# Moving the RMS scale of a hybrid decoder layer behind its input projection

## The chip, the cores and the metric

The kernel runs on one core of one Trainium2 chip. The metric is the device time of one execution in microseconds (us), the median of several runs. A profiled execution is one run with the hardware profiler on; its span goes from the first to the last instruction.

## The reference, cut to what matters

The input `x` has 2048 tokens of 1024 float32 values. What is computed:

```python
h = rmsnorm(x, norm_pre_g)                     # x * rsqrt(mean(x*x) + eps) * g, per token
z = einsum('bsd,de->bse', h, w_in)             # 1024 -> 4096 columns
q, k, v, g_attn, c_h, c_b, c_c, g_conv = split(z)   # 4 x 768, 4 x 256
q, k = rope(q, pos), rope(k, pos)              # 12 heads of 64
o = 3 dilated windows (128,1) (512,4) (2048,16), mixed by their softmax denominators
attn_out = o * silu(g_attn)
conv_out = c_b * causal_depthwise_conv(c_c * c_h, conv_w) * silu(g_conv)   # width 3
y = einsum('bse,ed->bsd', concat([attn_out, conv_out]), w_out)
out = x + rmsnorm(y, norm_post_g)
```

The RMS factor is one number per token, so it can be applied to `h` before the projection or to each column of `z` after it.

## The kernel before, in words

**Arithmetic.** float32 operands are split into a high part (the float32r cast) and a low part (the rest); a product is three matmuls, high·high, high·low, low·high.

**Tiling.** The tokens are cut into 4 chunks `b` of 512 tokens. The 4096 columns are cut into 8 groups of 512: group 0 and group 7 are convolution groups (c_h, c_c, c_b, gate, 128 columns each), groups 1 to 6 are attention groups (k, q, v, gate of two heads). A unit `n` is one group and one chunk, so there are 32 units, `n = 4 * group + b`: units 0 to 3 and 28 to 31 are convolution units, units 4 to 27 attention units. A unit's projection fills four PSUM tiles `z` (tokens along the free dimension) with 96 matmuls of 512 columns (L816 to L818).

**Start.** `x_chunk(b)` loads four tiles of 128 tokens (L417, 512 KB each), sums their squares on ScalarE (L419), takes the reciprocal root, multiplies the tile by it on VectorE (L428 for chunk 0, L435 for the others), and transposes it on TensorE (L443) into eight tiles; ScalarE writes the high part (L448), VectorE the low part (L450) of `xt`. These are also written to DRAM (L453) and read again for each later group (L459). `weights_in` loads 256 KB of weights (L396, L400) into one of three `raw` tiles and splits them (L403, L404).

**An attention unit.** ScalarE copies k and q out of PSUM (L520); four small transfers each swap the halves of the heads (L523); `rotate` multiplies by the rotary table `cs` (L535, read by L515 into a ring of one buffer) and adds (L539); the results are split (L545, L546 for k; L550, L551 for q). ScalarE copies v out of PSUM (L527), TensorE transposes it (L567). `silu2` takes the gate from PSUM: Tanh on ScalarE (L465), then `(tanh + 1) * z` on VectorE (L466). Scores (L604, L632), maxima and exponentials (L611, L615, L639, L643), transposes of the probabilities (L657), their split (L662, L663), products with v (L676), gathering (L694 to L696), weights over the windows (L742 to L758), and the mixed result `m` (L780 to L783) that goes to DRAM (L784).

**A convolution unit** copies c_h to `hh` (L481) and c_b to `bb` (L490), makes `u = z * hh` (L482), runs the three taps (L492, L494), multiplies by `bb` (L496, GpSimd) and by the gate (L497), and writes the result (L499).

**Output stage.** When all attention results are written, the attention buffers are given up (`open_out`), w_out is loaded (L855) and split (L857, L858), the mixed results are loaded (L867) and split (L868, L869) and projected (L883 to L885). The loads land in 12 tiles: 4 `uu`, 3 `raw` and 5 `ro`.

**Order.** `add(engine, duration, priority, function, reads, writes)` only records an operation. `Plan.schedule` plays all of them through with estimated durations and latencies: an engine that is free takes the ready operation with the smallest priority number whose buffers are free. `URG` marks evictions that go first. Then each engine gets its instructions in the planned order, which is fixed, and all transfers go through the one queue of SP in planned order. A `Ring` gives its buffers in the order in which they were asked for in the code.

## Time and profile before

| what | value |
|---|---|
| time before, median of 3 runs | 1248.66 us (1248.54 to 1251.12) |
| profiled execution, its own time | 1251.67 us |
| span of the profiled execution | 1249.9 us |
| mean granted TensorE clock | 0.992 |
| busy: TensorE, weight loads, VectorE, ScalarE, GpSimd | 1216.9, 1010.9, 826.6, 704.5, 252.5 us |

A busy share is an average over stages. Matmuls are pipelined, so a busy TensorE is not one at its peak; what counts is where its queue waits. Releasers ("<-") are inferred from semaphore events. PE is TensorE, PEld its weight loads, DVE VectorE, ACT ScalarE, POOL GpSimd, SP the engine whose queue issues the transfers (SPq).

### The profile page before, as it was taken

The numbers are of one execution on the slowest core, as the hardware profiler recorded it, in microseconds if no ns is written. First come the engines' busy times: TensorE is split into PE (matmuls) and PEld (weight loads), VectorE is DVE, ScalarE is ACT, GpSimd is POOL, SyncE is SP. The second block draws the span as 40 slices with busy tenths as digits, with TensorE's granted clock in tenths as the row PEclk, the third lists the DMA queues.
The fourth block names the chain that finished last, engine by engine and source line by source line (L and its number), as shares of the span: only waits on it lengthen the run. The fifth ranks groups of instructions, "written<-read, shape, count | busy, mean of one in ns | idle before, by whom it ended". The sixth has DMA issues, their size and how long they took to land.

```text
span 1249.9 us, 20939 instructions
## 1 busy us (share of the span) xinstructions
PE 1216.9 (97%) x6920; PEld 1010.9 (81%) x6920; DVE 826.6 (66%) x2124; ACT 704.5 (56%) x1856; POOL 252.5 (20%) x204
## 2 busy tenths in 40 slices
PE   6999999999999999999999999999999998999997
PEld 5888788888887888888887888888887886788886
DVE  6554367877788777877788677876787535444343
ACT  6533366766776766766766766767665614232121
POOL 0000132322322222322223222312232111000000
PEclk9999899999999999999999999999999999899999
DMA  9847666765777656765777656765778458553331
GB/s 350 326 189 294 227 207 193 248 195 165 240 236 264 222 189 218 241 204 156 239 246 264 214 176 216 262 197 161 233 241 277 131 171 328 186 167 119 101 101 67
DMA packets 137244, 264.39 MB, mean 212 GB/s; under 512 B 31280, under 2 KB 71344, under 8 KB 137136
## 3 DMA queue, kind: packets, MB, share of 16 engines
q1 hardware_dynamic: 137136, 263.07, 63.5%
q8 instruction: 54, 0.88, 0.3%
q14 instruction: 54, 0.44, 0.1%
HBM read 202.51 MB, written 47.91 MB: 200 GB/s over the span
## 4 chain that ended last, share of the span: by engine, by line
PE 83%; DVE 7%; ACT 4%; DMA 2%; issue 2%; SPq 1%; POOL 1%; DVEq 0%; ACTq 0%; POOLq 0%
PE z L816 15%; PE z L818 14%; PE z L817 14%; PE st L676 6%; PE st L657 6%; PE st L884 5%; PE st L885 5%; PE st L883 5%; PE st L604 4%; PE st L632 3%; PE st L443 1%; PE st L816 1%; PE st L818 1%; DVE rp L535 1%; PE st L817 1%
## 5 line engine op out<-in xcount | busy, mean ns | idle before, releaser
L816 PE MATMUL z<-xt,w 128*128 128x512 f32 x960 | 396.7, 413 | 0.0
L818 PE MATMUL z<-xt,w 128*128 128x512 f32 x960 | 376.9, 393 | 0.0
L817 PE MATMUL z<-xt,w 128*128 128x512 f32 x960 | 376.0, 392 | 0.0
L818 PEld LDWEIGHTS z<-xt,w 128*128 128x128 f32 x960 | 180.5, 188 | 41.4
L816 PEld LDWEIGHTS z<-xt,w 128*128 128x128 f32 x960 | 181.1, 189 | 32.2 <-issue 3.0
L817 PEld LDWEIGHTS z<-xt,w 128*128 128x128 f32 x960 | 181.4, 189 | 26.9
L663 DVE TENSOR_TENSOR pt<-st,pt 128x512 fp32r<-128x512 f32 x216 | 142.7, 679 | 57.1 <-ACT pt L662 56.1
L662 ACT CAST pt<-st 128x512 fp32r<-128x512 f32 x216 | 120.2, 579 | 32.4 <-PE st L657 30.3
L676 PEld LDWEIGHTS st<-pt,v 128*128 128x128 f32 x852 | 121.0, 189 | 17.7 <-issue 5.5
L676 PE MATMUL st<-pt,v 128*128 128x256 f32 x852 | 131.7, 285 | 2.4 <-DVE pt L663 2.4
L615 ACT ACTIVATE p<-p,sm 128x128 f32<-128x128 f32 (+3 forms) x192 | 105.7, 553 | 46.4 <-DVE sm L611 46.4
L696 DVE TENSOR_TENSOR uu<-st,uu 64x256 f32<-64x256 f32 x192 | 80.2, 421 | 73.4 <-ACT uu L695 63.8
L657 PE MATMUL st<-cst,p 128*128 128x128 f32 x852 | 122.6, 273 | 0.0
L725 POOL TENSOR_TENSOR uu<-uu 128x512 f32<-128x512 f32 x48 | 67.1, 1398 | 238.3 <-DVE uu L696 238.3
L657 PEld LDWEIGHTS st<-cst,p 128*128 128x128 f32 x852 | 100.5, 140 | 16.7 <-issue 1.5
L643 ACT ACTIVATE p<-p,e 128x256 f32<-128x256 f32 (+1 forms) x192 | 94.8, 497 | 26.3 <-DVE e L639 26.3
L694 ACT COPY uu<-st 64x256 f32<-64x256 f32 x192 | 70.3, 368 | 66.2 <-PE st L676 59.4
L889 ACT ACTIVATE y<-st 128x512 f32<-128x512 f32 x32 | 19.1, 598 | 133.0 <-PE st L885 133.0
L611 DVE CUSTOM_DVE_ANT_0 p<-st,cst 128x128 f32<-128x128 f32 (+3 forms) x192 | 82.1, 486 | 11.1 <-PE st L604 11.0
L639 DVE CUSTOM_DVE_ANT_0 p<-st,cst 128x256 f32<-128x256 f32 (+1 forms) x192 | 66.8, 410 | 21.3 <-PE st L632 21.3
L884 PE MATMUL st<-wo,w 128*128 128x512 f32 x192 | 76.1, 396 | 0.0
L883 PE MATMUL st<-wo,w 128*128 128x512 f32 x192 | 75.8, 395 | 0.0
(135 smaller groups left out, 1763.5 us busy)
## 6 DMA issues: line engine op xcount, KB each, us to landing
xt<-xt SPq DMA_DIRECT2D x256, 512.0 KB, 5.8
raw<-in_w_in SPq DMA_DIRECT2D x64, 256.0 KB, 5.7
cs<-in_rope SPq DMA_DIRECT2D x24, 512.0 KB, 6.4
rp<-rp SPq DMA_DIRECT2D x192, 64.0 KB, 2.0
vd<-v SPq DMA_DIRECT2D x96, 128.0 KB, 4.8
v<-vd SPq DMA_DIRECT2D x24, 512.0 KB, 4.1
ab<-ad SPq DMA_DIRECT2D x48, 256.0 KB, 6.0
mix<-m SPq DMA_DIRECT2D x32, 256.0 KB, 2.2
```

The lines of the kernel that those rows point to most:

```text
L611: add("DVE", dvet(w) + 0.01, pr + URG, lambda h=h, r=r, P4=P4: vec.tensor_tensor_reduce(P4.ap[:, r, 0:w], ps[h].ap[:, (r - r0) * w:(r - r0 ...
L615: add("ACT", actt(w) + 0.19, pr, lambda h=h, r=r, P4=P4: act.activation(P4.ap[:, r, 0:w], P4.ap[:, r, 0:w], AF.Exp, bias=s4(0, h)[:, r:r + ...
L643: add("ACT", actt(256 - lo[g]) + 0.19, pr, lambda h=h, g=g, P1=P1: act.activation(P1.ap[:, g, lo[g]:], P1.ap[:, g, lo[g]:], AF.Exp, bias=E ...
L657: nc.tensor.transpose(ps.ap[:, i * 128:(i + 1) * 128], pp.ap[:, a, c * 128:(c + 1) * 128], ident)
L662: add("ACT", actt(m * 128, True), pr + URG, lambda: act.copy(pt.ap[:, :m, 0, :], p4()), r=[ps], w=[(pt, 0)])
L663: add("DVE", dvet(m * 128), pr + URG, lambda: vec.tensor_tensor(pt.ap[:, :m, 1, :], p4(), f(pt.ap[:, :m, 0, :]), op=ALU.subtract), r=[ps, ...
L676: mm(dst, v, pt.ap[:, i], start=s, stop=e)
L816: mm(z.ap, w.ap[:, 0, js], xt.ap[:, 0], start=kt == 0, stop=False)
L817: mm(z.ap, w.ap[:, 0, js], xt.ap[:, 1], start=False, stop=False)
L818: mm(z.ap, w.ap[:, 1, js], xt.ap[:, 0], start=False, stop=kt == KT - 1)
L883: mm(z.ap, m.ap[:, 0, il], wo[:, 0, dl], start=e == 0, stop=False)
L884: mm(z.ap, m.ap[:, 0, il], wo[:, 1, dl], start=False, stop=False)
```

## The change

The projection takes `x * g` without the RMS factor. Tiles of x are transposed as they land. Chunk 0 is loaded in eight halves of 256 KB, first the columns of the first four transposes, behind the identity and the first weights. The squares are summed later; the factor of 512 tokens is spread over the 128 partitions by four transposes of a broadcast column (`spread`) and stands as a third plane of the table `t`; the rotary planes are multiplied by it. The table of a chunk goes to DRAM (`t_d`, 768 KB) and is read again for every later unit. In the units v, the gate, c_h and c_b are multiplied by the plane on VectorE as they leave PSUM, `u` once more on GpSimd. `silu2` writes the scaled gate, takes Tanh from it into an `rp` tile, and multiplies. The first eight weights land in `raw`, `rp` and `g` tiles. `g` has three tiles instead of two, `m` none: mixed results are written over the gates. The output stage's loads land in `uu`, `raw`, `rp` and `g` (14 tiles) instead of 12. The ring `sm` has three tiles instead of four.

```diff
+    t_d = [dram.tile([128, 3, C], F32, name=f"t{b}") for b in range(NB)]
...
-    g_r = ring(cp, "g", 2, [128, C])
+    g_r = ring(cp, "g", 3, [128, C])
-    m_r = ring(cp, "m", 2, [128, C])
+    raw0_r = Ring(list(raw_r) + list(rp_r) + list(g_r)[:1])
...
-    cs_r = ring(ap_, "cs", 1, [128, 2, C], F32, "STREAM")
+    cs_r = ring(cp, "cs", 1, [128, 3, C], F32, "STREAM")
-    sm_r = ring(ap_, "sm", 4, [128, 64])
+    sm_r = ring(ap_, "sm", 3, [128, 64])
-    junk = cs_r[0].ap.rearrange("p a b -> p (a b)")
+    junk = ab_r[0].ap.rearrange("p a b c -> p (a b c)")
...
-        pr = (4 * grp - 1) * 100 + 50 + 6 * i if grp else -150 + 5 * i
-        raw, w = Tok(raw_r), Tok(wp_r)
+        pr = (4 * grp - 1) * 100 + 50 + 6 * i if grp else -150 + 5 * i if i else -161
+        pc = pr if grp else URG + (-150 + 5 * i if i < 4 else 45.6 + i)
+        raw, w = Tok(raw_r if grp else raw0_r), Tok(wp_r)
-        add("ACT", actt(C), pr, lambda: act.copy(w.ap[:, 0], raw.ap), r=[raw], w=[(w, 0)])
-        add("DVE", dvet(C) + 0.07, pr, lambda: vec.tensor_tensor(w.ap[:, 1], raw.ap, f(w.ap[:, 0]), op=ALU.subtract),
+        add("ACT", actt(C), pc, lambda: act.copy(w.ap[:, 0], raw.ap), r=[raw], w=[(w, 0)])
+        add("DVE", dvet(C) + 0.07, pc, lambda: vec.tensor_tensor(w.ap[:, 1], raw.ap, f(w.ap[:, 0]), op=ALU.subtract),
             r=[raw, (w, 0)], w=[(w, 1)], after=XL[i - 1:i] if grp == 0 and i else ())
...
-    XT, XL = {}, []
     def x_chunk(b):
-        pr = b * 100 - 60 if b else -200
+
         xn = []
-        root = Tok(sm_r) if b else None
+        root, tp, t = Tok(sm_r), Tok(st_r), Tok(cs_r)
+        T[b] = t
         for i in range(4):
-            t = Tok(xs_r)
-            rows = slice(b * C + i, (b + 1) * C, 4)
-            add("DMA", dmat(512), b * 100 - 160 + i, lambda t=t, rows=rows: nc.sync.dma_start(t.ap, x[rows]), w=[t])
-            s, k = (root, i) if b else (Tok(sm_r), 0)
-            add("ACT", actt(D), pr + i, lambda t=t, s=s, k=k: act.activation(junk, t.ap, AF.Square, accum_out=s.ap[:, k:k + 1]),
-                r=[t], w=[(s, k), "junk"])
-            if b == 0:
-                add("ACT", 0.2, pr + i, lambda s=s: act.activation(s.ap[:, 3:4], s.ap[:, 0:1], AF.Sqrt, bias=eps, scale=1.0 / D),
-                    r=["eps", (s, 0)], w=[(s, 3)])
-                add("DVE", 0.07, pr + i, lambda s=s: vec.tensor_scalar(
-                    s.ap[:, 1:2], s.ap[:, 0:1], 1.0 / D, EPS, op0=ALU.mult, op1=ALU.add), r=[(s, 0)], w=[(s, 1)])
-
-                def norm(t=t, s=s):
-                    vec.tensor_scalar(t.ap, t.ap, rsqrt_root(s.ap), None, op0=ALU.mult)
-                add("DVE", 1.5, pr + i, norm, r=[s], w=[t])
-            xn.append(t)
-        if b:
-            after = XL[4:5] if b == 1 else ()
-            add("DVE", 2.6, pr + 4, lambda: rsqrt_mean(root.ap), w=[root], after=after)
-            for i, t in enumerate(xn):
-                add("DVE", 0.75, pr + 4 + i, lambda i=i, t=t: vec.tensor_scalar(
-                    t.ap, t.ap, root.ap[:, 8 + i:9 + i], None, op0=ALU.mult), r=[root], w=[t])
+            xn.append(Tok(xs_r))
+        rows = [slice(b * C + i, (b + 1) * C, 4) for i in range(4)]
+        for h in range(2):
+            for i, z in enumerate(xn):
+                pr = -160 + h * 7 + i if b == 0 else b * 100 - 160 + i
+                if b == 0:
+                    add("DMA", dmat(256), pr, lambda z=z, i=i, h=h: nc.sync.dma_start(
+                        z.ap[:, h * C:(h + 1) * C], x[rows[i], h * C:(h + 1) * C]), w=[(z, h)], land=4.0)
+                elif h == 0:
+                    add("DMA", dmat(512), pr, lambda z=z, i=i: nc.sync.dma_start(z.ap, x[rows[i]]), w=[(z, 0), (z, 1)])
...
             pos = 8 * b + kt - 4
-            p2 = pos // 8 * 100 + 49.5 + pos % 8 if pos >= 0 else -100 + kt
-            xpre = add("PE", 0.44, p2, tr, r=xn + ["cst"], w=[ps, (s, "hold")])
-            x_last.append(xpre)
+            p2 = pos // 8 * 100 + 49.5 + pos % 8 if pos >= 0 else -152 + 5 * kt
+            x_last.append(add("PE", 0.44, p2, tr, r=[(z, kt // 4) for z in xn] + ["cst"], w=[ps, (s, "hold")]))
...
-            add("DMA", dmat(512), p2 + 60, lambda kt=kt, s=s: nc.sync.dma_start(xt_d[b][kt], f(s.ap)), r=[s], w=[("xt", b, kt)])
+            add("DMA", dmat(512), max(p2, -50) + 60, lambda kt=kt, s=s: nc.sync.dma_start(xt_d[b][kt], f(s.ap)), r=[s], w=[("xt", b, kt)])
+        pr = b * 100 - 40
+        for i, z in enumerate(xn):
+            x_last.append(add("ACT", actt(D), pr + i, lambda i=i, z=z: act.activation(junk, z.ap, AF.Square, accum_out=root.ap[:, i:i + 1]),
+                              r=[z], w=[(root, i), "junk"], after=XL[3:4]))
+        pr += 8
+        add("DVE", 2.6, pr, lambda: rsqrt_mean(root.ap), w=[root])
+
+        def spread():
+            for i in range(4):
+                nc.tensor.transpose(tp.ap[:, i * 128:(i + 1) * 128], root.ap[:, 8 + i:9 + i].to_broadcast([128, 128]), ident)
+        add("PE", 0.44, pr, spread, r=[root, "cst"], w=[tp, (t, "hold")])
+        add("ACT", actt(C, True), pr + URG, lambda: act.copy(t.ap[:, 2], tp.ap), r=[tp], w=[(t, 2)])
+        add("DMA", dmat(512), b * 100 - 50, lambda: nc.sync.dma_start(t.ap[:, 0:2], rope[b]), w=[(t, 0)])
+        for i in range(2):
+            add("DVE", dvet(C), pr + 10, lambda i=i: vec.tensor_tensor(t.ap[:, i], t.ap[:, i], t.ap[:, 2], op=ALU.mult), r=[(t, 2)], w=[(t, 0)])
+        add("DMA", dmat(768), pr + 60, lambda: nc.sync.dma_start(t_d[b], t.ap), r=[t], w=[("t", b)])
+
+    T = {}
 
     def x_stream(n, kt):
...
-    def silu2(z, pr):
-
-        g = Tok(g_r)
-        add("ACT", actt(C, True), pr, lambda: act.activation(g.ap, z.ap, AF.Tanh, scale=0.5), r=[z], w=[g])
-        add("DVE", dvet(C) + 0.07, pr, lambda: vec.scalar_tensor_tensor(g.ap, g.ap, 1.0, z.ap, op0=ALU.add, op1=ALU.mult),
-            r=[z], w=[g])
+    def silu2(z, t, pr):
+
+        g, th = Tok(g_r), Tok(rp_r)
+        add("DVE", dvet(C), pr, lambda: vec.tensor_tensor(g.ap, z.ap, t.ap[:, 2], op=ALU.mult), r=[z, t], w=[g])
+        add("ACT", actt(C), pr, lambda: act.activation(th.ap, g.ap, AF.Tanh, scale=0.5), r=[g], w=[th])
+        add("DVE", dvet(C) + 0.07, pr, lambda: vec.scalar_tensor_tensor(g.ap, th.ap, 1.0, g.ap, op0=ALU.add, op1=ALU.mult),
+            r=[th], w=[g])
         return g
+
+    def table(b, prio):
+
+        t = Tok(cs_r)
+        add("DMA", dmat(768), prio, lambda: nc.sync.dma_start(t.ap, t_d[b]), r=[("t", b)], w=[t])
+        return t
...
-        hh, bb, y, m = Tok(rp_r), Tok(rp_r), Tok(rp_r), Tok(m_r)
-        add("ACT", actt(C, True), pe, lambda: act.copy(hh.ap, zs[0].ap), r=[zs[0]], w=[hh])
+        t = table(b, pr - 100) if i else T[b]
+        hh, bb = Tok(rp_r), Tok(rp_r)
+        add("DVE", dvet(C), pe, lambda: vec.tensor_tensor(hh.ap, zs[0].ap, t.ap[:, 2], op=ALU.mult), r=[zs[0], (t, 2)], w=[hh])
         add("DVE", dvet(C), pe, lambda: vec.tensor_tensor(
             u.ap[:, 2:].rearrange("p r i -> p (r i)"), zs[1].ap, hh.ap, op=ALU.mult), r=[zs[1], hh], w=[(u, 1)])
+        add("POOL", poolt(C), pe, lambda: pool.tensor_tensor(
+            u.ap[:, 2:].rearrange("p r i -> p (r i)"), u.ap[:, 2:].rearrange("p r i -> p (r i)"), t.ap[:, 2], op=ALU.mult), r=[t], w=[(u, 1)])
 
...
-        add("ACT", actt(C, True), pe, lambda: act.copy(bb.ap, zs[2].ap), r=[zs[2]], w=[bb])
-        g = silu2(zs[3], pe)
+        add("DVE", dvet(C), pe, lambda: vec.tensor_tensor(bb.ap, zs[2].ap, t.ap[:, 2], op=ALU.mult), r=[zs[2], (t, 2)], w=[bb])
+        g = silu2(zs[3], t, pe)
+        y = Tok(rp_r)
...
-        add("DVE", dvet(C) + 0.07, pr, lambda: vec.scalar_tensor_tensor(m.ap, y.ap, 0.5, g.ap, op0=ALU.mult, op1=ALU.mult),
-            r=[y, g], w=[m])
-        add("DMA", dmat(256), pr, lambda: nc.sync.dma_start(mix_d[6 + i][b], m.ap), r=[m], w=[("mix", 6 + i, b)])
+        add("DVE", dvet(C) + 0.07, pr, lambda: vec.scalar_tensor_tensor(g.ap, y.ap, 0.5, g.ap, op0=ALU.mult, op1=ALU.mult),
+            r=[y], w=[g])
+        add("DMA", dmat(256), pr, lambda: nc.sync.dma_start(mix_d[6 + i][b], g.ap), r=[g], w=[("mix", 6 + i, b)])
...
-        cs = Tok(cs_r)
-        add("DMA", dmat(512), pr - 100, lambda: nc.sync.dma_start(cs.ap, rope[b]), w=[cs], after=x_last)
+        cs = table(b, pr - 100)
...
-        add("ACT", actt(C, True), pe + 2, lambda: act.copy(vz.ap, zs[2].ap), r=[zs[2]], w=[vz])
-        gs = silu2(zs[3], pe + 3)
+        add("DVE", dvet(C), pe + 2, lambda: vec.tensor_tensor(vz.ap, zs[2].ap, cs.ap[:, 2], op=ALU.mult), r=[zs[2], cs], w=[vz])
+        gs = silu2(zs[3], cs, pe + 3)
...
-        add("POOL", poolt(C), pr, lambda: pool.tensor_tensor(m.ap, a4.ap, gs.ap, op=ALU.mult), r=[a4, gs], w=[m])
-        attn_last.append(add("DMA", dmat(256), pr, lambda: nc.sync.dma_start(mix_d[p][b], m.ap), r=[m], w=[("mix", p, b)]))
+        add("POOL", poolt(C), pr, lambda: pool.tensor_tensor(gs.ap, a4.ap, gs.ap, op=ALU.mult), r=[a4], w=[gs])
+        attn_last.append(add("DMA", dmat(256), pr, lambda: nc.sync.dma_start(mix_d[p][b], gs.ap), r=[gs], w=[("mix", p, b)]))
...
-    add("DMA", 0.5, -156.5, lambda: nc.sync.dma_start(ident, consts[:, 0:128]), w=["cst"])
-    add("DMA", 1.2, 0, lambda: nc.sync.dma_start(cst[:, 128:], consts[:, 128:]), w=["masks"])
-    add("DMA", 0.5, -156.4, lambda: nc.sync.dma_start(gp, g_pre), w=["gp"])
+    add("DMA", 0.5, -165, lambda: nc.sync.dma_start(ident, consts[:, 0:128]), w=["cst"])
+    add("DMA", 0.5, -156.5, lambda: nc.sync.dma_start(gp, g_pre), w=["gp"])
+    add("DMA", 1.2, 200, lambda: nc.sync.dma_start(cst[:, 128:], consts[:, 128:]), w=["masks"])
     add("DMA", 0.5, -100, lambda: nc.sync.dma_start(cw, conv_w), w=["cw"])
-    for b in range(NB):
-        x_chunk(b)
     for n in range(8 * NB):
         grp, b = divmod(n, NB)
+        if n < NB:
+            x_chunk(b)
...
-    ro_r = Ring([Slot() for _ in range(5)])
-    or_r = uu_r + raw_r + ro_r
+    or_r = uu_r + raw_r + rp_r + g_r
```

## Rows read from the trace of the kernel before

**Rows 1.** The page, busy time of each engine over the span.
```profile
PE 1216.9 (97%) x6920; PEld 1010.9 (81%) x6920; DVE 826.6 (66%) x2124; ACT 704.5 (56%) x1856; POOL 252.5 (20%) x204
```

**Rows 2.** Busy time by stretch: the stretch in us, its length, busy us of PE, PEld, DVE, ACT and POOL with their instructions, granted clock, DMA share, GB/s.
```profile
125.00:150.00 25.00, 23.12 (x116) 18.85 (x114) 9.41 (x33) 8.46 (x29) 5.08 (x4) 0.86 0.74 257
...
600.00:800.00 200.00, 198.57 (x1240) 166.10 (x1237) 153.62 (x418) 138.91 (x387) 51.82 (x43) 1.00 0.68 219
...
1050.00:1100.00 50.00, 42.74 (x175) 34.14 (x174) 24.08 (x50) 17.97 (x37) 2.81 (x1) 0.90 0.61 215
```

**Rows 3.** Waits of TensorE's matmuls over the whole span: who waited for whom, us in total, times, longest.
```profile
PE st L883 <- ACT mx L868: 4.4, 1, 4.4
PE st L885 <- DVE mx L869: 2.9, 1, 2.9
PE st L604 <- DVE q L551: 2.6, 5, 0.6
PE st L567 <- ACT rp L527: 2.5, 2, 1.9
```

**Rows 4.** The chain of waits in the first 17 us, in order of time: start, us, what.
```profile
0.74 4.07 DMA p<-in_x
4.83 1.16 ACT cs L419 x2
...
11.85 0.77 DVE p L428
...
12.66 3.46 PE st L443 x17
16.12 0.23 PE z L816
```

**Rows 5.** The timeline at the start: start, us, engine, line, operation, tiles, count, idle before and releaser. Two lines of SP's queue and TensorE's first transposes.
```profile
0.74 1.81 SPq L417 DMA_DIRECT2D p<-in_x  x4
2.59 0.66 SPq L791 DMA_DIRECT2D cst<-in_consts  x1
...
8.98 1.04 PE L443 MATMUL st<-cst,p 128*128 128x128 f32 x2 [8.98 <-DMA cst<-in_consts]
```

**Rows 6.** What the transfers moved in the first 20 us, in 40 slices of 0.5 us.
```profile
GB/s 0 0 0 106 49 295 360 410 426 418 434 401 410 442 370 370 379 406 389 390 382 401 393 328 393 385 410 369 418 401 434 391 416 420 428 393 426 434 410 410
```

**Rows 7.** The chain of waits from 0 to 40 us: one group of four transposes of x once the projection runs.
```profile
18.86 0.44 PE st L443 x4
```

**Rows 8.** Single lines over the whole span: engine, operation, count, duration in ns as least/median/most, first and last start, shape.
```profile
L663 DVE TENSOR_TENSOR pt<-st,pt x216: 545/691/694, 152.6 to 999.2; 128x512 fp32r<-128x512 f32 x108
L466 DVE SCALAR_TENSOR_TENSOR g<-g,z x24: 677/687/690, 141.0 to 953.5; 128x512 f32<-128x512 f32 x24
L535 DVE TENSOR_TENSOR rp<-rp,cs x72: 651/691/1802, 131.1 to 940.9; 128x512 f32<-128x512 f32 x72
L539 POOL TENSOR_TENSOR rp<-rp,rp x24: 1288/1542/1782, 137.7 to 942.3; 128x512 f32<-128x512 f32 x24
L527 ACT COPY rp<-z x24: 579/587/590, 139.9 to 952.2; 128x512 f32<-128x512 f32 x24
L419 ACT ACTIVATE cs<-p x12: 1038/1058/1080, 4.8 to 58.6; 128x1024 f32<-128x1024 f32 x12
L419 ACT ACTIVATION_READ_ACCUMULATOR cs<-p x12: 182/186/223, 5.8 to 59.5; 128x1 f32 x12
```

**Rows 9.** The timeline where the scores of the second attention unit of a group of four begin: start, us, engine, line, idle before and releaser.
```profile
597.65 0.59 ACT L527 COPY rp<-z 128x512 f32<-128x512 f32 x1
597.66 1.11 DVE L551 TENSOR_TENSOR q<-rp,q 128x512 fp32r<-128x512 f32 x1 [1.33 <-ACT q L550]
...
598.80 0.69 DVE L466 SCALAR_TENSOR_TENSOR g<-g,z 128x512 f32<-128x512 f32 x1
...
598.83 0.62 PE L604 MATMUL st<-kk,q 64*128 64x256 f32 x6 [0.52 <-DVE q L551]
```

**Rows 10.** The timeline at the end of the first attention unit's projection.
```profile
138.26 0.39 PE L818 MATMUL z<-xt,w 128*128 128x512 f32 x1
...
139.36 0.62 ACT L550 CAST q<-rp 128x512 fp32r<-128x512 f32 x1 [5.58 <-POOL rp L539]
139.89 0.58 ACT L527 COPY rp<-z 128x512 f32<-128x512 f32 x1
...
140.52 0.66 PE L567 MATMUL st<-cst,rp 128*128 128x128 f32 x4 [1.88 <-ACT rp L527]
```

**Rows 11.** The rotary table: the page's row of its transfers (KB each, median us from issue to landing), and SP's queue from one unit's load to the next unit's swaps.
```profile
cs<-in_rope SPq DMA_DIRECT2D x24, 512.0 KB, 6.4
...
595.18 0.38 SPq L515 DMA_DIRECT2D cs<-in_rope  x1
...
615.62 2.45 SPq L523 DMA_DIRECT2D rp<-rp  x4
```

**Rows 12.** The beginning of the output stage: SP's queue, and two lines of ScalarE's timeline.
```profile
1033.13 0.38 SPq L850 DMA_DIRECT2D gpost<-in_g_post  x1
1040.25 0.32 SPq L499 DMA_DIRECT2D mix<-m  x1
1040.62 2.34 SPq L855 DMA_DIRECT2D ro<-in_w_out  x5
...
1055.16 0.59 ACT L481 COPY rp<-z 128x512 f32<-128x512 f32 x1 [3.70 <-PE z L818]
```

More of the change, by code (lines that the diff above doesn't have):

```diff
@@ L315, in hybrid_layer @@
     cw = cp.tile([128, 2, 3], F32, name="cw")
-    eps = cp.tile([128, 1], F32, name="eps")
-    eps2 = cp.tile([128, 1], F32, name="eps2")
+    t_d = [dram.tile([128, 3, C], F32, name=f"t{b}") for b in range(NB)]
     xt_d = [[dram.tile([128, 2, C], F32, name=f"xt{b}_{k}") for k in range(KT)] for b in range(NB)]
@@ L405, in weights_in @@
             r=[raw, (w, 0)], w=[(w, 1)], after=XL[i - 1:i] if grp == 0 and i else ())
-    XT, XL = {}, []
+    XT, XL, x_last = {}, [], []
     def x_chunk(b):
-        pr = b * 100 - 60 if b else -200
         xn = []
-        root = Tok(sm_r) if b else None
+        root, tp, t = Tok(sm_r), Tok(st_r), Tok(cs_r)
+        T[b] = t
         for i in range(4):
-            t = Tok(xs_r)
-            rows = slice(b * C + i, (b + 1) * C, 4)
-            add("DMA", dmat(512), b * 100 - 160 + i, lambda t=t, rows=rows: nc.sync.dma_start(t.ap, x[rows]), w=[t])
-            s, k = (root, i) if b else (Tok(sm_r), 0)
-            add("ACT", actt(D), pr + i, lambda t=t, s=s, k=k: act.activation(junk, t.ap, AF.Square, accum_out=s.ap[:, k:k + 1]),
-                r=[t], w=[(s, k), "junk"])
-            if b == 0:
-                add("ACT", 0.2, pr + i, lambda s=s: act.activation(s.ap[:, 3:4], s.ap[:, 0:1], AF.Sqrt, bias=eps, scale=1.0 / D),
-                    r=["eps", (s, 0)], w=[(s, 3)])
-                add("DVE", 0.07, pr + i, lambda s=s: vec.tensor_scalar(
-                    s.ap[:, 1:2], s.ap[:, 0:1], 1.0 / D, EPS, op0=ALU.mult, op1=ALU.add), r=[(s, 0)], w=[(s, 1)])
-                def norm(t=t, s=s):
-                    vec.tensor_scalar(t.ap, t.ap, rsqrt_root(s.ap), None, op0=ALU.mult)
-                add("DVE", 1.5, pr + i, norm, r=[s], w=[t])
-            xn.append(t)
-        if b:
-            after = XL[4:5] if b == 1 else ()
-            add("DVE", 2.6, pr + 4, lambda: rsqrt_mean(root.ap), w=[root], after=after)
-            for i, t in enumerate(xn):
-                add("DVE", 0.75, pr + 4 + i, lambda i=i, t=t: vec.tensor_scalar(
-                    t.ap, t.ap, root.ap[:, 8 + i:9 + i], None, op0=ALU.mult), r=[root], w=[t])
@@ L452, in x_chunk @@
                 r=[ps, "gp", (s, 0)], w=[(s, 1)]))
-            add("DMA", dmat(512), p2 + 60, lambda kt=kt, s=s: nc.sync.dma_start(xt_d[b][kt], f(s.ap)), r=[s], w=[("xt", b, kt)])
-    x_last = []
+            add("DMA", dmat(512), max(p2, -50) + 60, lambda kt=kt, s=s: nc.sync.dma_start(xt_d[b][kt], f(s.ap)), r=[s], w=[("xt", b, kt)])
[15 more added lines that the diff above has]
+    T = {}
     def x_stream(n, kt):
@@ L777, in weight @@
             return ab.ap[:, i].rearrange("p g (r j) -> p g r j", r=4)
-        a4, a1, m = UU[4][0], UU[1][0], Tok(m_r)
+        a4, a1 = UU[4][0], UU[1][0]
         add("DVE", dvet(C), pr, lambda: vec.tensor_tensor(rows(a4), rows(a4), weight(1), op=ALU.mult), r=[ab], w=[a4])
@@ L837, in open_out @@
         for s, t in zip(xr_r, ring(op_, "xr", 2, [128, D])):
-            s.ap = t.ap
-        for s, t in zip(ro_r, ring(op_, "ro", 5, [128, C])):
             s.ap = t.ap
```

2 lines of the change are left out of this document (removed).

## The prediction

> **What bounds the kernel now.** I read the busy times first, then the busy times by stretch, then TensorE's waits, and last the chain of waits at the places where the waits lie. TensorE is busy for 97% of the span [rows 1], which alone says little, since its matmuls are pipelined; but its waits over the whole span are short and few: the longest are 4.4, 2.9, 2.6 and 2.5 us in total, 12.4 us of 1249.9 [rows 3]. In a stretch of 200 us amid the attention units TensorE shows 198.57 us, VectorE 153.62 (77%) and ScalarE 138.91 (69%) [rows 2]. So TensorE's queue sets the time from its first projection to the end, and three places lie outside that: the head, where the first projection starts only at 16.12 us [rows 4]; the first attention unit, where the granted clock of the stretch falls to 0.86 [rows 2, 10]; and the beginning of the output stage with 7.3 us of waits and a granted clock of 0.90 [rows 2, 3]. An edit pays only if it shortens one of these or takes instructions off TensorE; work on other engines costs nothing until TensorE waits for it.
>
> **The head: the largest term.** Before, the chain is: x lands at 4.81 us; squares, root and product of one tile after another; the last product at 11.85; then the transposes from 12.66, 17 in 3.46 us, and the projection at 16.12 [rows 4]. The change takes squares, root and products out of it. What is left is the landing of four half tiles. Ahead of the last of them SP issues the identity (64 KB), 256 KB of weights and three halves, with it 1.376 MB. The slices of the first 20 us sum to 1.376 MB at 5.8 us [rows 6]; the first tile's 0.524 MB were moved by 3.8 us and counted as landed at 4.81, 1.0 us later [rows 4, 6]. That gives 6.8 us; the identity takes 0.66 us to issue and now stands first [rows 5], so I take 7.0. The fourth transpose then starts at 7.0 instead of 12.66: **-5.7 us**. Bound below 6.7 us (-6.0); bound above the 8.98 us at which TensorE's first transpose ran before, released by the identity, which stood behind 2.1 MB of x [rows 5] (-3.7). The transposes, projections and splits behind it are the same work. The weights don't spoil it: all eight can now land without waiting for a tile, and the second of them is the 2.69th MB, moved by 9.1 us [rows 6]; landed and split it is there before 12.4, when the projection, begun at 9.6 (13 more transposes of 3.46/17 = 0.20 us [rows 4]), has used the first (12 matmuls of 0.23 us [rows 4]).
>
> **Added to TensorE.** Four transposes per chunk spread the factor: 0.44 us per group of four [rows 7], four chunks, **+1.8 us** on an engine without slack. The first group waits for the root of chunk 0, and the transposes and projections stand behind it in TensorE's queue. The plan reckons 0.95 us for a sum of squares; the rows show 1.06 and 0.19 for reading the sum [rows 8], so four of them are 1.2 us late against the plan. I take half, **+0.6** (bounds 0 and 1.2).
>
> **Added to VectorE.** Each attention unit gets two more products: v (0.59 us on ScalarE before) and the gate, each 0.69 us by the nearest rows with one PSUM operand [rows 8], while Tanh and the last product of the gate stay. That is 24 x 1.38 = 33 us on an engine that is 77% busy, so on the average it hides behind TensorE, which has the next unit's projection to run. It shows only where VectorE is ahead of TensorE on the path: from k and q to the scores. In the unit shown, q's low part starts at 597.66, scores wait for it, and v leaves PSUM at 597.65 [rows 9]; v and gate come to stand at VectorE just when q's low part does. TensorE waited there 5 times [rows 3]. Six units (one in four) with the first product ahead in half of the cases: 6 x 0.69 x 0.5 = **+2.1**. Bound below: the 2.6 us of these waits gone (-2.6); bound above: both products ahead in 12 units, +16.6.
>
> One detail of the silu: its last product read one PSUM operand and never took more than 0.690 us; now both operands lie in SBUF, as in L535, which takes up to 1.802 us beside 0.691 in the median [rows 8]. The Trainium skill's GPSIMD Engine Reference, section Specifications, says that GpSimd and VectorE contend for SBUF where VectorE has two SBUF inputs; the rows bear it out, 0.694 at most with a PSUM operand and 1.802 with two in SBUF. By the rule, if all 24 met GpSimd, VectorE would get 27 us more; by the median nothing. The gate is wanted only at the unit's end, so I take nothing on the path.
>
> **The first attention unit.** TensorE waits 1.88 us for v's copy, which stands on ScalarE behind q's cast, which waits for GpSimd; v's `z` was done at 138.65 [rows 10]. VectorE takes v now and would be done by 139.3 instead of 140.5: **-1.2** (bounds 0 and -1.9).
>
> **Costed at nothing.** The table: its load grows from 512 to 768 KB and the 6.4 us of landing to perhaps 9, and it can be issued only when gate and v of the unit before have been read as well. From one unit's load to the next unit's swaps 20 us pass [rows 11], so some 9 us stay; without that cover v, gate and the rotations wait, and with them the three `z` tiles. Gates over results: three tiles against two and two, one unit's worth less; a result is read by its transfer within a few us. The `rp` ring gives a sixth tile per unit to Tanh; the next unit's k waits for it, but that comes 10 us later. The conv units: c_h, c_b and gate move to VectorE, 0.69 us each, while the `z` tiles of a unit finish three matmuls of 0.23 us apart, so `z` tiles come free as soon. The rotary load and the writing of the tables (5 MB) fall in the first 100 us, beside a solid projection. The output stage: two more landing tiles, but shared with units 30 and 31: 0, bounds -5 and +5 (half of the ten us lost there each way).
>
> **The sum.** -5.7 + 1.8 + 0.6 + 2.1 - 1.2 = -2.4 us against the profiled execution's 1251.67 (span 1249.9), that is 1249.3. The median of the runs is 3.0 us below the profiled one, so 1248.66 - 2.4 = **1246.3 us**.
>
> **Rivals.**
> 1. *Two more products on VectorE decide (slower).* Mechanism as above: v and gate go out ahead of q's low part, and scores start later. Price 1.38 us per unit that pays both; in all six units 8.3 us instead of 2.1, 1252.5; in 12 units 16.6, 1260.8. The other terms are -4.5, so the gain is gone from the fourth unit on that pays both. For it: the times in [rows 9] coincide to 0.01 us. Against: TensorE has other work planned into such gaps, and only 2.6 us of such waits exist now. Chance 0.16.
> 2. *The output stage gets shorter.* The w_out loads stood behind a result of unit 30 in SP's queue from 1033.5 to 1040.25, and ScalarE's splits behind the end of unit 31's projection until 1055.16 [rows 12]; the waits of 7.3 us come from that [rows 3]. A conv result is ready later in the plan now (one more product on GpSimd, 1.3 to 1.8 us [rows 8]), so some w_out loads go ahead of it, and 14 tiles hold more. Half of the loss: -5, 1241.3. Chance 0.20.
> 3. *The same place gets longer (slower).* w_out loads take the `rp` and `g` tiles at the boundary of units 30 and 31; the evictions wait for a split, TensorE for `z`. One landing, about +5: 1251.3. Chance 0.07.
> 4. *The halves don't help as much.* The last first half lands at the 8.98 us of the upper bound: 2 us less, 1248.3. The Trainium skill's page DMA: Bandwidth & Descriptors (section Bandwidth) says that small transfers are inefficient, 138 GB/s at 64 KB and 341 at 1 MB; interpolated to 256 KB and one after another that would be an estimated 11.6 us, a gain of 1.1 and 1250.9 in all. The trace disagrees: some 410 GB/s with 256 KB loads in the queue [rows 6]. Chance 0.07.
>
> **How the numbers follow.** A difference under 0.2% (2.5 us) can't be told from no change. The forecast's own case (1243 to 1249) has 0.5, of which a little over half, 0.27, lies below 1246.2. Rival 2 adds 0.20 to faster, rival 4 0.07 to same; rivals 1 and 3 are slower, 0.23. So faster 0.47, same 0.30, slower 0.23. The range goes from 1239 (rival 2, and the two small waits of the first root and of the scores gone, -2.7) to 1255 (rival 1 in some eight units); the likeliest case by itself is 1243 to 1249.
>
> **What would show it.** The first projection at 10 us or a little before, and transposes from about 7; no squares ahead of it on ScalarE; at 100 us the last transposes of x some 4 us earlier than before; waits of TensorE for L551's line of 3 to 6 us; no long wait for v in the first attention unit; VectorE some 33 us busier in the attention units. The prediction is wrong if TensorE's waits for VectorE grow beyond 7 us, if the first projection starts after 12 us, or if the gap before the output projection changes by more than 5 us.

## The result: 1238.0 us, and most of it from a part that was costed at nothing

The changed kernel takes 1238.02 us (median, 1235.51 to 1239.90) against 1249.89 us of the kernel before on the same chip: ratio 0.9902, 95% interval 0.9876 to 0.9929. The forecast was 1246.3 with a range from 1239 to 1255: the direction was right, the size was not, and the median lies 1 us below the range. The profiled executions are 1238.0 and 1249.9 us long, 11.9 us apart, and both have the clock dip of [rows 2] at 125 to 150 us, so they can be compared event by event.

TensorE's waits after, over the whole span (who waited for whom, us in total, times, longest); the rows of before are [rows 3], and one row of before that [rows 3] leaves out stands below them:

```profile
PE st L432 <- DMA p<-in_x: 7.3, 3, 5.2
PE st L690 <- DVE pt L677: 5.8, 7, 1.2
PE st L581 <- DVE rp L541: 1.5, 1, 1.5
PE st L894 <- DVE mx L878: 1.4, 1, 1.4
PE st L618 <- ACT q L564: 0.3, 1, 0.3
PE st L618 <- DVE q L565: 0.2, 1, 0.2
```

```profile
PE st L676 <- DVE pt L663: 2.4, 6, 0.8
```

The 4.4 and 2.9 us ahead of the output projection have become 1.4; the waits of the scores for q's low part, which were to grow from 2.6 to between 3 and 6, have become 0.2. One kind of wait grew: the products with v (L676 before, L690 now) wait for the split probabilities on VectorE for 5.8 us instead of 2.4. The same stretches as in [rows 2] (PE, PEld, DVE, ACT, POOL busy, granted clock, DMA share, GB/s):

```profile
125.00:150.00 25.00, 23.53 (x130) 19.12 (x129) 12.07 (x44) 8.78 (x31) 5.11 (x4) 0.86 0.76 265
600.00:800.00 200.00, 198.50 (x1237) 166.33 (x1236) 154.34 (x427) 138.20 (x384) 59.26 (x45) 1.00 0.71 225
1050.00:1100.00 50.00, 48.56 (x213) 39.59 (x212) 28.59 (x60) 18.39 (x38) 2.57 (x2) 1.00 0.61 216
```

The third row is the news: in the output stage TensorE is busy for 48.56 of 50 us instead of 42.74, at a granted clock of 1.00 instead of 0.90. And the head, by the chain of waits (start, us, what), against [rows 4]:

```profile
3.06 5.71 DMA p<-in_x
...
8.82 3.89 PE st L432 x17
12.71 0.43 PE z L828
```

Where the 11.9 us lie is seen from the start of the same events in both traces, and in four of the runs told below (us; u is VectorE's product `u = z * hh` of a conv unit, the square is ScalarE's third of the output stage, where the waits are over):

| event | before | after | in place alone | z late | no spread | after again |
|---|---|---|---|---|---|---|
| u of unit 0 | 41.7 | 37.9 | 41.6 | 37.3 | 36.9 | 36.4 |
| u of unit 3 | 114.9 | 113.4 | 115.3 | 112.8 | 111.0 | 112.0 |
| u of unit 31 | 1055.9 | 1053.2 | 1052.3 | 1052.0 | 1048.4 | 1051.1 |
| third square | 1084.2 | 1072.3 | 1070.1 | 1075.6 | 1067.4 | 1070.2 |

From before to after: 3.8 us are gained up to unit 0, 2.3 are given back over the other chunks, the attention and conv units bring another 1.2 in this pair (more on it below), and then 9.2 us are gained between unit 31 and the output stage. Everything ahead of the output stage adds up to -2.7 us, where the forecast had -2.4. Nearly the whole miss is the term of the output stage: 0 was taken, 9.2 was measured.

### The profile page after: what moved, and what is told of

Its sections match the earlier page's. It is cut to its first block, busy times and chain, and to the rows that moved or that the text cites. A ratio compares the mean times of both kernels' runs of the same rounds, so it can differ in the third digit from the quotient of the medians.

```text
span 1238.0 us, 21038 instructions
## 1 busy us (share of the span) xinstructions
PE 1214.2 (98%) x6936; PEld 1010.8 (82%) x6936; DVE 839.7 (68%) x2179; ACT 688.7 (56%) x1814; POOL 277.7 (22%) x212
## 4 chain that ended last, share of the span: by engine, by line
PE 90%; DVE 3%; issue 2%; ACT 2%; DMA 1%; SPq 1%; POOL 1%; DVEq 0%; POOLq 0%; ACTq 0%
PE z L828 16%; PE z L830 16%; PE z L829 16%; PE st L690 7%; PE st L671 7%; PE st L893 5%; PE st L892 5%; PE st L894 5%; PE st L618 4%; PE st L646 3%; PE st L432 1%; PE st L828 1%; PE st L829 1%; PE st L830 1%; PE st L581 1%
## 5 line engine op out<-in xcount | busy, mean ns | idle before, releaser
L676 ACT CAST pt<-st 128x512 fp32r<-128x512 f32 x216 | 119.6, 580 | 33.7 <-PE st L671 31.5
L690 PEld LDWEIGHTS st<-pt,v 128*128 128x128 f32 x852 | 119.9, 189 | 21.3 <-issue 6.4
L690 PE MATMUL st<-pt,v 128*128 128x256 f32 x852 | 129.4, 285 | 6.1 <-DVE pt L677 5.8
L739 POOL TENSOR_TENSOR uu<-uu 128x512 f32<-128x512 f32 x48 | 71.5, 1490 | 210.3 <-DVE uu L710 210.1
L796 POOL TENSOR_TENSOR uu<-uu 128x512 f32<-128x512 f32 x24 | 33.2, 1382 | 277.1 <-DVE uu L795 277.1
L653 DVE CUSTOM_DVE_ANT_0 p<-st,cst 128x256 f32<-128x256 f32 (+1 forms) x192 | 66.8, 412 | 16.6 <-PE st L646 16.5
L893 PE MATMUL st<-wo,w 128*128 128x512 f32 x192 | 75.6, 394 | 0.0
```

The source lines that it names most:

```text
L676: add("ACT", actt(m * 128, True), pr + URG, lambda: act.copy(pt.ap[:, :m, 0, :], p4()), r=[ps], w=[(pt, 0)])
L690: mm(dst, v, pt.ap[:, i], start=s, stop=e)
L893: mm(z.ap, m.ap[:, 0, il], wo[:, 1, dl], start=False, stop=False)
```

## The experiments

Theory Q was the first: SP's queue. Before, the w_out loads all stand behind unit 30's result [rows 12]; after, seven go ahead of it (SP's queue after):

```profile
1016.90 0.32 SPq L798 DMA_DIRECT2D mix<-g  x1
...
1021.79 0.60 SPq L859 DMA_DIRECT2D gpost<-in_g_post  x1
1024.09 0.32 SPq L463 DMA_DIRECT2D xt<-xt  x1
1024.46 0.90 SPq L864 DMA_DIRECT2D raw<-in_w_out  x2
...
1029.90 1.86 SPq L864 DMA_DIRECT2D uu<-in_w_out  x4
...
1038.87 0.33 SPq L514 DMA_DIRECT2D mix<-g  x1
```

Theory T was the tiles that the loads land in. The first four runs try both, each from both sides.

**The stage opened behind unit 30's result, in the changed kernel.**

```diff
+        conv_last.append(add("DMA", dmat(256), pr, lambda: nc.sync.dma_start(mix_d[6 + i][b], g.ap), ...
...
-    gate = add("DMA", 0.0, 3300, open_out, after=attn_last, w=["open"])
+    gate = add("DMA", 0.0, 3300, open_out, after=attn_last + conv_last[6:7], w=["open"])
```

> The changed kernel with one wait more: the output stage opens only when the result of unit 30 has been written, so that no w_out load stands ahead of that result in SP's queue, as in the kernel before. Theory Q (the queue's order made the 9.2 us at the output stage): TensorE's waits at the start of the output projection come back, 6 to 9 us, with a granted clock under 1 there, and the time is some 9 us above the changed kernel's 1238, about 1247. Rival T (the 14 landing tiles made it): the waits stay near the 1.4 us of the changed kernel, 1238 to 1240. Rival H (the shift comes from the head and the attention units): no change but noise, 1238.

Measured: 1253.87 us (1.0045 of before, 1.003 to 1.006), slower than before. TensorE waits 11.4 and 2.9 us ahead of the output projection and the clock of 1050 to 1075 us is 0.73:

```profile
PE st L893 <- ACT mx L878: 11.4, 1, 11.4
```

So when the stage opens is worth the whole gain and more. This run doesn't tell what opens it earlier.

**Unit 30's result behind the w_out loads, in the kernel before.**

```diff
-        add("DMA", dmat(256), pr, lambda: nc.sync.dma_start(mix_d[6 + i][b], m.ap), ...
+        add("DMA", dmat(256), 3311 if n == 30 else pr, lambda: nc.sync.dma_start(mix_d[6 + i][b], m.ap), ...
```

> The kernel before with one priority changed: the transfer of unit 30's result stands behind the sixteen w_out loads in SP's queue instead of ahead of them. Theory Q: the loads start at 1033.5 us instead of 1040.6; TensorE's waits at the start of the output projection fall from 7.3 to 0 to 3 us, the time by 6 to 9 us, about 1242. Rivals T and H: 1249, waits of 7.3 us as before.

Measured: 1247.39 us, 0.9997 (0.9988 to 1.0007). The loads start at 1029 instead of 1040 us, but the waits stay at 3.8 and 3.3 us. Theory Q as it stood, the one transfer in front, falls: with it gone, six of the 16 splits still stand behind unit 31's evictions on ScalarE.

**Landing tiles of their own in the changed kernel, and shared ones in the kernel before.**

```diff
-    or_r = uu_r + raw_r + rp_r + g_r
+    ro_r = Ring([Slot() for _ in range(3)])
+    or_r = uu_r + raw_r + ro_r
```

(10 tiles instead of 14; the second run has the reverse: `uu_r + raw_r + rp_r + g_r`, 13 tiles, in the kernel before.)

> The changed kernel, its output loads landing in 10 tiles (4 uu, 3 raw, 3 of their own) instead of the 14 that take in the rp and g tiles. Theory Q: the loads keep their place in the queue, so the time stays within 2 us of the changed kernel's 1238. Rival T: with fewer tiles than the 12 of before the waits of 7.3 us come back, 1245 or more.

> The kernel before, its output loads landing in 13 tiles (uu, raw, rp and g) instead of 12 with five of their own. Theory Q: the loads stand behind unit 30's result as before, waits of 7.3 us, 1249 as before within 2. Rival T: waits fall to some 1.4 us, 1241. A loss by sharing tiles with units 30 and 31 would show as waits of TensorE for z at their boundary.

Measured: 1239.88 us (0.9936, 0.9922 to 0.9951) and 1247.76 us (0.9997, 0.9987 to 1.0006). The waits stay at 1.4 us in the one and at 4.4 and 2.5 us in the other. Theory T falls.

**Results in the place of the gates, alone, in the kernel before.** A row that was there to be read in the trace of before led on: the gates of the conv units whose `z` lies in an `st` tile, over the whole span, and the one of unit 29 in ScalarE's timeline (start, us, engine, line, idle before and releaser):

```profile
L465 ACT ACTIVATE g<-st 128x512 f32<-128x512 f32 x8 | 4.7, 590 | 4.6 <-DVE m L497 4.6
```

```profile
1018.86 0.60 ACT L465 ACTIVATE g<-st 128x512 f32<-128x512 f32 x1 [4.63 <-DVE m L497]
```

Unit 29's Tanh waits 4.6 us for L497, the product that makes unit 28's result and is the last to read its gate: there are two gate tiles, and the last attention unit's gate sits in the other. (A ring serves requests in order, each from the tile that the plan has free first.) Until the Tanh has run, unit 29's fourth `z` stays taken.

```diff
-    g_r = ring(cp, "g", 2, [128, C])
+    g_r = ring(cp, "g", 3, [128, C])
...
-    m_r = ring(cp, "m", 2, [128, C])
...
-        add("POOL", poolt(C), pr, lambda: pool.tensor_tensor(m.ap, a4.ap, gs.ap, op=ALU.mult), r=[a4, gs], w=[m])
+        add("POOL", poolt(C), pr, lambda: pool.tensor_tensor(gs.ap, a4.ap, gs.ap, op=ALU.mult), r=[a4], w=[gs])
```

> The kernel before with one part of the change alone: three gate tiles, and the mixed result written in place of the gate (no result tiles). Theory A (gate tiles): before, unit 29's Tanh waits for one of two gate tiles, held by the results of units 27 and 28; its z tile stays taken, the fourth z of unit 30's projection comes late, the x tiles it holds come free in one bunch, unit 31's loads go out in one bunch behind it on SP, and the output stage opens late. Then this part alone takes away most of the 9 us: 1239 to 1241 us, waits before the output projection 0 to 3 us instead of 7.3, w_out loads from about 1025 us. Theory B (the evictions moved from ScalarE to VectorE, or the earlier head, open the stage): the time stays at 1247 to 1249 us and the waits at 6 us or more.

Measured: 1237.82 us, 0.9917 (0.9904 to 0.993). By its time this one part gives nearly what the whole change gives (10.7 us by the medians beside it). The Tanh comes 1.7 us behind the unit's u product instead of 6.5, so its wait is gone; the other 3.6 us by which it runs earlier have another cause, since this execution has no clock dip at 125 to 150 us (granted clock 1.00 there, 0.86 in the profiled kernel before). No wait of the output projection is left in the list, and its stretch is full. First before (the stretch; the u product of unit 29, to be read with its Tanh at 1018.86 above), then this run:

```profile
1050.00:1075.00 25.00, 17.74 (x65) 13.62 (x64) 16.52 (x30) 13.34 (x26) 2.81 (x1) 0.80 0.96 337
...
1012.39 0.69 DVE L482 TENSOR_TENSOR u<-z,rp 128x512 f32<-128x512 f32 x1 [6.02 <-PE z L818]
```

```profile
1008.79 0.69 DVE L481 TENSOR_TENSOR u<-z,rp 128x512 f32<-128x512 f32 x1 [6.03 <-PE z L817]
...
1010.53 0.58 ACT L464 ACTIVATE g<-st 128x512 f32<-128x512 f32 x1
...
1050.00:1075.00 25.00, 25.00 (x111) 20.56 (x110) 13.52 (x28) 10.49 (x21) 2.82 (x1) 1.00 0.74 263
```

**The same part undone in the changed kernel** (two gate tiles, one result tile, in the same space).

> The changed kernel with that part undone within the same space: two gate tiles and one result tile, results no longer in place. Theory A as the only cause: the waits before the output projection come back, 1244 to 1247 us. Theory A with the moved evictions as a second cover (a gate's z tile is read by one product instead of Tanh and a product): the fourth z of unit 30 is late by three steps instead of eighteen, and 1 to 4 us come back: 1239 to 1242 us. Theory B: no change, 1237 to 1239 us.

Measured: 1240.58 us (1238.06 to 1243.44), 0.9941 (0.9926 to 0.9956): by the intervals hardly told from the changed kernel. The wait grows from 1.4 to 3.4 us. So the part is enough but not needed. The gate's `z` is still taken late here: the product that reads it waits for unit 27's result, which is the last reader of its gate tile, and comes 6.0 us behind unit 29's u (1005.83 us), against 1.2 in the changed kernel. But only 10 steps go ahead of the first into unit 30's fourth `z`, where the kernel before has 18 (shown with the late fourth `z` below):

```profile
1011.83 0.69 DVE L470 TENSOR_TENSOR g<-st,cs 128x512 f32<-128x512 f32 x1 [1.38 <-POOL m L798]
```

This is the smaller delay that the second case of its expectation has. That it is smaller because one product reads the `z`, where Tanh and a product did, is argued; no run undoes both parts together.

**The third gate tile without results in place, in the kernel before** (three gate tiles, one result tile).

> The kernel before with three gate tiles and one result tile instead of two and two, results still written to their own tile. If the third gate tile alone ends the chain (unit 29's Tanh need not wait for unit 28's result): 1238.5 to 1241 us and waits before the output projection of 0 to 4 us. If it needs the result in the gate's place too: the one result tile makes the Tanh or the product wait as before, 1245 to 1249 us.

Measured: 1240.11 us, 0.9931 (0.992 to 0.9942), 1.0 us of waits left, clock 1.00 from 1050 to 1075 us. The tile does most of it: 9.1 us by the medians beside it.

**The late fourth `z`, put back into the changed kernel.**

```diff
-              add("PE", 3 * (mmt(C) + 0.003), n * 100 + 50 + (kt if conv else ...), proj, ...
+              add("PE", 3 * (mmt(C) + 0.003), n * 100 + 50 + (5.5 + kt / 10 if n == 30 and j == 3 and kt < 6 else kt if conv else ...), proj, ...
```

> The changed kernel with one order put back: in unit 30's projection the matmuls into the fourth z tile come behind eighteen steps of the other three, as they stand before (nothing waits for a tile; the sum of work is the same). If the x tiles held by that order are the link between the gate tiles and the output stage: unit 31's loads go out in one bunch on SP again, and the first output projection's waits grow from 1.4 to 4 to 8 us, 1240 to 1246 us. If the order costs nothing by itself: 1236 to 1239 us and 1.4 us of waits.

Measured: 1242.5 us (1240.46 to 1244.74), 0.9944 (0.993 to 0.9958). The link can be read in two kernels. Before, in unit 30's projection (matmuls of one line, their tiles, first and last start), 18 steps go into the three `z` tiles before the first into the fourth, which is `st`:

```profile
L816 PE MATMUL z<-xt,w x18: 389/389/389, 1013.5 to 1025.0; 128*128 128x512 f32 x18
```

Each step is needed by all four, so none of the x tiles comes free until the fourth `z` has had its turn, and unit 31's x loads then go out in a bunch, ahead of everything for the output stage (SP's queue of before):

```profile
1026.60 0.32 SPq L459 DMA_DIRECT2D xt<-xt  x1
1027.01 0.38 SPq L499 DMA_DIRECT2D mix<-m  x1
1027.48 5.55 SPq L459 DMA_DIRECT2D xt<-xt  x6
```

With the order put back, the changed kernel shows the same bunch and 3.3 and 0.5 us of waits:

```profile
1022.64 6.44 SPq L463 DMA_DIRECT2D xt<-xt  x7
```

```profile
PE st L894 <- DVE mx L878: 3.3, 1, 3.3
...
PE st L892 <- ACT mx L877: 0.5, 1, 0.5
```

From unit 31 to the output stage it is 4.5 us longer than the changed kernel run again (1052.0 to 1075.6 against 1051.1 to 1070.2). The order by itself is about half of the 9.2 us. The other half isn't isolated by a run; in this one the stage still opens early (two w_out loads at 1018.94 us, ahead of the bunch), which it doesn't do before.

**Whole tiles of chunk 0.** Four loads of 512 KB instead of eight halves.

> The changed kernel with chunk 0 loaded in four whole tiles of 512 KB instead of eight halves. If the halves are worth what the bytes say (1 MB less ahead of the last transpose's tile at 340 GB/s and more, of which the slices behind a transfer give 2.5 to 3.0 us): the first steady transposes from 11.5 us instead of 8.8, 1240.5 to 1241 us. If the small transfers cost the rate that the fewer bytes save: 8.8 to 9.5 us and within 1 us of the changed kernel.

Measured: 1245.14 us (1238.35 to 1246.09). In the profiled execution the steady transposes start at 9.80 us. Four of the seven runs lie within a microsecond of 1246, and the profiled one of these has a granted clock of 0.86 from 125 to 150 us and of 0.93 from 325 to 350 us. The changed kernel, with halves, shows the first of these dips in one execution and not in another (last section), so the dips don't come from the whole tiles alone. By the head the halves are worth 1 to 2.4 us (9.80 against 8.82 and 7.38 to 8.13), less than the bytes say; the time says nothing.

**The first weights behind the first halves.**

```diff
-        pr = (4 * grp - 1) * 100 + 50 + 6 * i if grp else -150 + 5 * i if i else -161
+        pr = (4 * grp - 1) * 100 + 50 + 6 * i if grp else -150 + 5 * i if i else -156.7
```

> The changed kernel with the first 256 KB of weights loaded behind the four first halves of x instead of ahead of them. If the landing goes by the bytes ahead: the fourth half lands 0.7 us earlier (256 KB at some 350 GB/s), the transposes run from 8.1 us, 1237.3 us. If it goes by a start-up that all transfers share: no change in the landing, 1238.0 us.

Measured: 1236.39 us (1235.92 to 1238.84), 0.9907 (0.9894 to 0.992). The steady transposes start at 6.91 us, in one execution:

```profile
6.91 3.72 PE L432 MATMUL st<-cst,p 128*128 128x128 f32 x16 [0.80 <-DMA p<-in_x]
```

**Four runs side by side:** the changed kernel again; v and gate off VectorE; no spread; a head by tiles.

> The changed kernel itself once more, so that the three runs beside it are compared on the same chip: 1236 to 1239 us.

> The changed kernel with the two products per attention unit taken off VectorE: v is copied by ScalarE and the gate's Tanh reads the projection's result itself, as before (the scale of v and of the gate in the attention units is left out of the computation). If the 33 us that VectorE got in these units hide behind TensorE: within 1.5 us of the changed kernel. If they sit in front of q's low part, as the prediction's term of 2.1 us and its first rival have it: 2 to 8 us faster than the changed kernel.

> The changed kernel without the 16 transposes on TensorE that spread the factor over the partitions (the third part of the table is filled with ones by ScalarE, so the scale is left out of the computation). If TensorE's queue has no slack there: 1.8 us faster than the changed kernel, 4 x 0.44 us. If the transposes fall into waits that are there anyway (the first projection's behind the landing, the first root's): 0 to 0.5 us.

> The changed kernel with the weights behind the first halves, the first 16 transposes in the order of the tiles that land instead of that of the columns, the transposes of the second halves behind the first projections, and the second weight tile ahead of the second halves. If the head is set by the last first half's landing and what TensorE has to do behind it: 12 transposes done before the fourth half lands at 6.9 us, first projection at 8.8 to 9.5 us instead of 12.7, all of it on TensorE's own queue, so some 2 us from the transposes' order on top of the 1.9 us from the weights: 1234 to 1235 us. If the evictions and splits behind the landing set it: first projection at 10.5 to 11 us, 1236 to 1237 us.

Measured: 1237.82 us (1234.58 to 1245.33; 0.991, 0.9887 to 0.9932), 1240.3 us (1238.41 to 1241.44), 1235.1 us (1234.46 to 1237.04) and 1238.67 us (1234.85 to 1241.19).

- Without the spread unit 3 comes 1.0 us earlier though unit 0 comes 0.5 later, 1.5 over three groups of 0.44 (the first group saves nothing that can be seen); the whole time is 2.7 us shorter, by medians whose intervals overlap. The 1.8 us is borne out in size.
- Without VectorE's two products unit 31 comes 2.4 us earlier (u at 1048.7), yet the median is 2.5 us longer (the intervals overlap): the output projection waits 4.3 us and its clock falls to 0.86 from 1050 to 1075 us, and unit 31 to the third square takes 25.0 us instead of 19.1. In the profiled execution the place that decides gave more back than the units had gained.

```profile
PE st L901 <- DVE mx L885: 4.3, 1, 4.3
```

- The head by tiles starts its projection at 8.68 us, as its first case has it (8.8 to 9.5), and unit 3 comes 1.3 us earlier than in the changed kernel run again; its profiled execution then loses that and more in dips at 125 to 150 us (0.86) and 325 to 350 us (0.93). The times do not separate it from the changed kernel. Nor do they the run with the weights behind. No version here is shown to beat the changed kernel.

## Why the prediction was wrong in size

- **Head, -5.7: mis-sized; measured -3.4.** The mechanism held: no squares or products stand ahead of the transposes. The fourth half was to land at 7.0 us, from bytes moved. In the profiled execution its transpose ran at 8.82, and in seven more executions with the same loads at 7.38 to 8.13. The rate was read from a queue of 512 KB loads: before moved 420 GB/s from 4 to 6 us and 398 from 6 to 8, the changed kernel 341 and 278. In the run with the 256 KB of weights behind the first halves it ran at 6.91. The fourth rival's landing, 8.98, is close to the profiled one; the 11.6 us estimated beside it by the Trainium skill's page DMA: Bandwidth & Descriptors, section Bandwidth, are far from all of them. Of the 2.3 us that are missing, 1.8 are this landing and 0.4 the transposes behind it, 17 as before but in 3.89 us instead of 3.46. The first projection was forecast at 9.6 with 13 transposes ahead of it, and a start after 12 us was named as a sign of being wrong; with 17, because a group of the second halves was ordered in front of it, it starts at 12.71.
- **Spread, +1.8: right in size**, by the run without it. **First root, +0.6:** no such wait stands in the list; 0. That the sum ahead of the output stage came out at -2.7 where -2.4 was forecast is luck: the head gave 2.3 us less than forecast, the attention and conv units 2.1 us more (-1.2 where 2.1 - 1.2 = +0.9 was forecast). And the -1.2 belongs to two executions that both have the clock dip. From u of unit 3 to u of unit 31 it takes 936.3 to 937.6 us in the four traced kernels with the attention units of before and no dip (unit 30 behind, shared tiles, in place alone, three gates), and 937.2 to 939.1 in five with the changed ones (stage opened late, own results, weights behind, no spread, after again): some 0.6 us longer, close to the forecast.
- **VectorE's two products, +2.1: not seen as forecast.** TensorE's waits for q's low part (L551 before, L565 now) are 0.2 us instead of 3 to 6: in the order that came out, q's low part stands ahead of v and gate. A price shows at another wait, that for the split probabilities: 2.4 us before, 5.8 now and 7.9 in the second run, but 3.4 without the two products (second run, then without the products):

```profile
PE st L690 <- DVE pt L677: 7.9, 8, 2.1
...
PE st L697 <- DVE pt L684: 3.4, 5, 1.6
```

  Nor did VectorE get 33 us busier in the attention units: from 150 to 985 us it is busy for 635.6 instead of 631.8 us, although the two products cost 16.5 and 16.2 us, as reckoned; others became shorter (last section). Without the products unit 31 comes 2.4 us earlier, about the size of the term; but the order of that whole run differs too, so the term isn't measured better than that. The first rival, that they decide, falls.
- **v in the first attention unit, -1.2: wrong.** The wait of 1.9 us [rows 10] is 1.5 us now. VectorE takes v, but behind q's low part (the timeline there):

```profile
137.16 0.69 DVE L565 TENSOR_TENSOR q<-rp,q 128x512 fp32r<-128x512 f32 x1 [1.83 <-ACT q L564]
...
137.77 0.68 DVE L541 TENSOR_TENSOR rp<-z,cs 128x512 f32<-128x512 f32 x1
...
138.51 0.66 PE L581 MATMUL st<-cst,rp 128*128 128x128 f32 x4 [1.47 <-DVE rp L541]
```

- **Output stage, 0 with bounds of 5 us each way: the step that failed.** Measured -9.2; a change of more than 5 us there was named as a sign of being wrong. The second rival had this side, half of the loss and a chance of 0.20, but by another mechanism: a later conv result on SP. The run that moved just that transfer brought nothing. The third, that landing tiles shared with units 30 and 31 make the place longer, isn't seen: shared tiles in the kernel before left its time at 0.9997. What failed in the text is "Gates over results: ... one unit's worth less", under "Costed at nothing": two rings of two were counted as tiles (four against three), where the question was whether a gate waits, and the row of L465 with 4.6 us of idle said that it does. The third gate tile alone brought 9.1 us to the kernel before; what covers the loss in the changed kernel without it stays open. The bound of 5 us, half of the ten lost, was no bound: it had no row that kept the other half.
- **The clock.** The stall before cost twice, the 7.3 us of waits and a granted clock of 0.80 from 1050 to 1075 us; with the waits at 1.4 us it is 1.00, with 3.8 us (late `z`) 0.93, and with 14.3 us (stage opened late) 0.73; but waits of 3.4 us (own results) left it at 1.00. Of the 9.2 us, 5.9 are waits; the other 3.3 fit the clock, by difference. Two runs bear that out, both counted from unit 31 to the third square against the 19.1 us of the changed kernel: with 2.0 us more of waits at 1.00 it takes 21.0, with 2.4 more at 0.93 it takes 23.6.

## What to carry to other kernels

Before an edit to a ring of tiles is costed at nothing, look for instructions that wait for a tile of it to be released, on the engines that seem idle: a wait of 4.6 us on ScalarE, off the chain, set the order of TensorE's work, and by that the loads, 30 us ahead of where TensorE stood still. In an order written out ahead, one late release moves everything queued behind it, so a stall is followed back through the queues to the first tile that was late, not to the transfer right in front. Where one boundary decides, gains ahead of it may be given back there: the run with 2.4 us less ahead of it was 2.5 us longer by its median.

## What the runs showed of the hardware

- The granted clock dips at the same places in some executions and not in others of the same kernel: 0.86 from 125 to 150 us (in the profiled changed kernel, not in its second run) and 0.93 from 325 to 350 us. The second run is 1.4 us ahead of the first before that stretch and 4.4 behind it (u of unit 3 at 113.4 and 112.0 us; k's eviction in the third attention unit at 188.8 and 184.4), so the first dip costs some 3 us.
- The same four first halves, behind the same loads, landed between 7.38 and 8.82 us in eight executions, a spread of 1.4 us, a quarter of the term that hung on it.
- With two products more per unit some other instructions of VectorE became shorter. One is the subtraction of q's low part (one line's count and its duration as least/median/most, before and after):

```profile
L551 DVE TENSOR_TENSOR q<-rp,q x24: 648/691/1784, 140.0 to 945.8; 128x512 fp32r<-128x512 f32 x24
```

```profile
L565 DVE TENSOR_TENSOR q<-rp,q x24: 671/693/805, 137.2 to 941.9; 128x512 fp32r<-128x512 f32 x24
```

The medians agree; the long ones, up to 1.78 us, are gone. They are not gone everywhere: the rotation's products (L535 in [rows 8], now L549) still take up to 1.80 us:

```profile
L549 DVE TENSOR_TENSOR rp<-rp,cs x72: 649/692/1803, 130.6 to 937.1; 128x512 f32<-128x512 f32 x72
```

Both operands of these instructions lie in SBUF. The Trainium skill's page SBUF — State Buffer, section Who interferes with whom, says that such an instruction of VectorE contends with one of GpSimd that reads SBUF. The traces agree: before, all six long ones of q's low part begin while an instruction of GpSimd is running and end 0.55 us after it, as this one:

```profile
378.54 1.78 POOL L725 TENSOR_TENSOR uu<-uu 128x512 f32<-128x512 f32 x1 [1.69 <-DVE uu L696]
...
379.10 1.78 DVE L551 TENSOR_TENSOR q<-rp,q 128x512 fp32r<-128x512 f32 x1
```

Seven others begin 0.03 us ahead of one of GpSimd and take 0.69. After, GpSimd's instruction has at most 0.26 us left when q's low part begins, and it takes at most 0.81. So the order of the two decides; no run here takes GpSimd's work away.
